# Two of eight channel blocks of a depthwise convolution moved from TensorE to VectorE, in small groups of taps

## The chip, the cores and the metric

The kernel runs on one core of a Trainium2 chip. The metric is the device time of one execution in microseconds (us); the median of three runs of the kernel before is 2086.12 us (2085.93 to 2087.42). TensorE (PE in the profile, PEld for its weight loads) multiplies matrices, VectorE (DVE) and ScalarE (ACT) work element by element, SyncE (SP) issues the DMA transfers.

## The reference

One inference step of a small decoder: a prompt of 512 positions and 8 sample sequences of 8 positions each, 1024 channels, all in float32. The change concerns the convolution module, the first layer:

```python
def conv_module(x, prev, norm_g, w_in, b_in, w_dw, b_dw, ln_g, ln_b, w_out, b_out):
    u = rms_norm(x, norm_g)
    a = u @ w_in + b_in
    glu = a[..., :D_MODEL] * jax.nn.sigmoid(a[..., D_MODEL:])
    ext = jnp.concatenate([prev.astype(glu.dtype), glu], axis=1)
    c = lax.conv_general_dilated(ext, w_dw[:, None, :].astype(ext.dtype), window_strides=(1,),
                                 padding='VALID', dimension_numbers=('NWC', 'WIO', 'NWC'),
                                 feature_group_count=D_MODEL) + b_dw
    h = jax.nn.silu(layer_norm(c, ln_g, ln_b))
    return h @ w_out + b_out, ext[:, -(CONV_WIDTH - 1):]
```

A depthwise convolution of 31 taps: every output channel is a sum of 31 shifted copies of its own input channel, each times a weight of the channel, plus a bias. A layer norm over the channels follows. After this layer come a feed-forward part, an attention layer over three dilated windows and a second feed-forward part; the change leaves them as they are.

## The kernel before

Channels lie on partitions: 8 blocks c = 0 to 7 of 128 channels. The positions, 512 of the prompt and 64 of the samples, N = 576, lie along the free dimension. They are projected in two halves of 288 (`HN`).

The work around the change is one loop, `for c in range(1, KT + 1)` at L628, which overlaps block c's projection with block c-1's convolution. The order of the instructions on each engine is the order in which the code emits them; nothing reorders them later. An iteration emits:

- `diagonals(c)` (L546, VectorE): the 31 taps of block c as diagonal matrices of 32x32, for TensorE.
- `in_proj(c, 0)` (L511): the first half of the projection. It begins with `w_next` (L161), which has SyncE load a later weight (`w_load`, L122 and L125, 1 MB), issues one or two copies of cache data from DRAM to DRAM behind it (`bg_copy`, L184, 1 MB each), and splits the weight that has arrived into a high part on ScalarE (`whi`, L140, four instructions) and a low part on VectorE (`wlo`, L141, four). A weight load waits on SyncE's queue until the split before has released the buffer, and the copies behind it wait too. Then TensorE multiplies 2 x 24 times, first the gate, then the value, each into a bank of its own of accumulator memory (`inp`, two banks). ScalarE takes the sigmoid of the gate (`sg`, L529), VectorE adds the bias and multiplies (`ext`, L536). The sigmoid frees the gate's bank, `ext` the value's; the next half needs both.
- `samples(c - 1, 0, 16)` (L578): the convolution of the 64 sample positions. ScalarE writes 31 products (`prod`, L586 and L588), 16 here and 15 after the convolution; VectorE sums them when the last is there (L590).
- `conv(c - 1)` (L551): the prompt's convolution on TensorE, 124 matmuls of 32x32 by 32x512 in four row groups, each two instructions in the trace. Its four banks (`acc`) are copied to SBUF by ScalarE and VectorE (`ev`, L561 and L563).
- In iteration 3, `pilot()` (L592): the mean over the channels of blocks 0 and 1, a first estimate of the layer norm's mean. It is subtracted from every block ahead of the sums. Then the squares of these blocks on ScalarE (`square`, L604).
- From iteration 4 on, `sums` (L608): TensorE adds up an earlier block and its squares, for the layer norm.
- `in_proj(c, 1)`: the second half; its `ext` completes the input of `conv(c)`.
- `reduced(c - 1)` (L565): TensorE adds up the four row groups of the convolution, VectorE adds the bias and subtracts the pilot mean into `cT` (L571, L573, L574).

After the loop the layer norm is completed from the sums (L657 on), and the output projection follows.

Of the kernel before, what the change touches and what calls it, by code (L numbers as in the profile page):

```python
# [30 lines left out]
ALU = mybir.AluOpType  # L31
# [3 lines left out]
KT = 8  # L35
S = 512
NB = 8
T = 8
NS = NB * T
# [8 lines left out]
TAPS = 31  # L48
# [42 lines left out]
def trunk(ctx: ExitStack, tc: tile.TileContext, I, O, dbg=None):  # L91
    nc = tc.nc
# [64 lines left out]
    def w_work(n=100):  # L157
        for _ in range(min(n, len(parts))):
            parts.pop(0)()

    def w_next(lazy=False):  # L161
        w_work()
        while not wstate["ready"]:
            if not wstate["raw"]:
                w_load()
            w_split()
            w_work()
        r = wstate["ready"].pop(0)
        if not lazy:
            w_load()  # L170
        bg_copy()
        w_split()
        if not lazy:
            w_work()
        return r
# [41 lines left out]
    ones = const.tile([128, 128], F32, name="ones")  # L217
# [127 lines left out]
    def conv_layer():  # L345
        with ExitStack() as cx:
            big = cx.enter_context(tc.tile_pool(name="a_big", bufs=1))
            wk = cx.enter_context(tc.tile_pool(name="a_wk", bufs=2))
            def row(tag, name):
                return wk.tile([128, N], F32, tag=tag, name=name)  # L350
# [4 lines left out]
            wdT = big.tile([128, KT, TAPS], F32, name="wdT")  # L355
# [7 lines left out]
            with tc.tile_pool(name="a_ps0", bufs=1, space=PSUM, reuse_waits="tile") as ps:  # L363
# [11 lines left out]
                o = 0  # L375
# [19 lines left out]
                def xtile():  # L395
                    return ps.tile([128, 512], F32, tag="xp", name="xp", bufs=3)
# [4 lines left out]
                for r in range(5):  # L401
                    n = 128 if r < 4 else NS
# [25 lines left out]
                for r in range(5):  # L428
                    n = 128 if r < 4 else NS
                    dg = wk.tile([128, 128], F32, name="dg", bufs=4)  # L430
                    nc.vector.tensor_scalar(dg[:n], ident[:n], rn[:n, r:r + 1], None, op0=ALU.mult)
                    o = pr[:, 0, r * 128:(r + 1) * 128] if r < 4 else pr[:, 1, :NS]
                    nc.tensor.matmul(o, ones[:n], dg[:n, :n], start=r in (0, 4), stop=r in (3, 4))
                pt = xtile()
# [16 lines left out]
                for k in range(KT):  # L451
# [9 lines left out]
                    for i, pt in ((1, pg), (0, pa)):  # L461
                        for h in range(2):
                            c = slice(h * HN, (h + 1) * HN)
# [6 lines left out]
                pt = xtile()  # L470
# [4 lines left out]
                for k in range(0, KT, 2):  # L475
                    pt = xtile()
# [12 lines left out]
            def bank(tag, n):  # L489
                return ps.tile([128, 512], F32, tag=tag, name=tag, bufs=n)  # L490

            cv = cvx.enter_context(tc.tile_pool(name="a_cv", bufs=1))
            cT = cv.tile([128, KT, N], F32, name="cT")
            tails = cv.tile([128, KT, 96], F32, name="tails")
            pil = cv.tile([128, N], F32, name="pil")
            exf = [cv.tile([128, 30 + S], F32, name=f"ext{i}") for i in range(KT)]
# [3 lines left out]
            bdw = V["a_b_dw"]  # L500
# [5 lines left out]
            hs = [slice(h * HN, (h + 1) * HN) for h in range(2)]  # L506
            grp = [slice(32 * r, 32 * r + 32) for r in range(4)]
            SP = S - HN
            W, SG = {}, {}

            def in_proj(c, h):  # L511

                if h == 0:
                    SG[c] = row("a", "sg")
                if c:
                    if h == 0:
                        W[c] = w_next(lazy=c == KT - 1)
                    wh, wl = W[c]
                    pts = []
                    for i in (1, 0):  # L520
                        pt = bank("inp", 2)[:, :HN]
                        for k in range(KT):
                            mm3(pt, wh[:, k, i], wl[:, k, i], uh[:, k, hs[h]], ul[:, k, hs[h]], k == 0, k == KT - 1)
                        pts.append(pt)
                    pg, pa = pts
                else:
                    pg, pa = pg0[:, h], pa0[:, h]
                sg = SG[c][:, hs[h]]
                nc.scalar.activation(sg, pg, AF.Sigmoid, bias=V["a_b_in"][:, 8 + c:9 + c])  # L529
                e, b = exf[c], V["a_b_in"][:, c:c + 1]  # L530
                jobs = [(e[:, 30:30 + HN], pa, sg)] if h == 0 else [
                    (e[:, 30 + HN:], pa[:, :SP], sg[:, :SP]),
                    (exts[:, c, :, 30:], pa[:, SP:].rearrange("p (b t) -> p b t", b=NB),
                     sg[:, SP:].rearrange("p (b t) -> p b t", b=NB))]
                for o, x, g in jobs:
                    nc.vector.scalar_tensor_tensor(o, x, b, g, op0=ALU.add, op1=ALU.mult)  # L536
                if h:
                    nc.scalar.activation(tails[:, c, 0:30], e[:, S:], AF.Copy)
                    nc.scalar.activation(tails[:, c, 32:].rearrange("p (b t) -> p b t", b=NB), exts[:, c, :, 30:], AF.Copy)
# [6 lines left out]
            def diagonals(c):  # L546
                d = DG[c] = cv.tile([128, TAPS, 32], F32, name="dgs", bufs=2)
                nc.vector.tensor_mul(d, id32[:, None, :].to_broadcast([128, TAPS, 32]),
                                     wdT[:, c, :, None].to_broadcast([128, TAPS, 32]))

            def conv(c):  # L551
                acc = [bank("acc", 4) for _ in range(4)]
                for m in range(0, TAPS, 4):
                    for j in range(m, min(m + 4, TAPS)):
                        for r, g in enumerate(grp):
                            nc.tensor.matmul(acc[r][32 * (j - m):32 * (j - m) + 32], DG[c][g, j], exf[c][g, j:S + j],  # L556
                                             start=m == 0, stop=j + 4 >= TAPS)
                ev = EV[c] = cv.tile([128, 4, S], F32, name="ev")
                for r in range(4):
                    if r % 2:  # L560
                        nc.vector.tensor_copy(ev[:, r], acc[r])  # L561
                    else:
                        nc.scalar.activation(ev[:, r], acc[r], AF.Copy)  # L563

            def reduced(c):  # L565
                pt, ev = bank("red", 1), EV.pop(c)
                for r, g in enumerate(grp):
                    nc.tensor.matmul(pt[g], id32, ev[:, r], start=True, stop=True)
                o, b = cT[:, c, :S], bdw[:, c:c + 1]
                if c < 2:  # L570
                    nc.vector.tensor_scalar(o, pt, b, None, op0=ALU.add)  # L571
                else:
                    nc.vector.scalar_tensor_tensor(o, pt, b, pil[:, :S], op0=ALU.add, op1=ALU.subtract)  # L573
                    nc.vector.tensor_sub(cT[:, c, S:], cT[:, c, S:], pil[:, S:])  # L574
# [17 lines left out]
            def pilot():  # L592

                for h in range(2):
                    pt = bank("inp", 2)[:, :HN]
                    for k in range(2):
                        nc.tensor.matmul(pt, ones, cT[:, k, hs[h]], start=k == 0, stop=k == 1)
                    nc.scalar.activation(pil[:, hs[h]], pt, AF.Copy, scale=1.0 / 256)
                for k in range(2):
                    nc.vector.tensor_sub(cT[:, k], cT[:, k], pil)  # L600

            SQ, STB = {}, []

            def square(c):  # L604
                SQ[c] = wk.tile([128, N], F32, tag="sq3", name="sq", bufs=3)
                nc.scalar.activation(SQ[c], cT[:, c], AF.Square)

            def sums(c):  # L608

                if not STB:  # L610
                    STB.append(bank("stat", 1))
                sq = SQ.pop(c)
                for q, x in enumerate((cT[:, c, :S], sq[:, :S], cT[:, c, S:], sq[:, S:])):
                    nc.tensor.matmul(STB[0][grp[q], :S if q < 2 else NS], ones[:, :32], x, start=c == 0, stop=c == KT - 1)

            def state_rows(hf):
                pt = bank("inp", 2)
# [4 lines left out]
                for a, n, d in ((0, 30, O["conv_state_prompt"][0, 0]), (32, 64, O["conv_state_sample"][0, :, 22:30])):  # L622
                    nc.sync.dma_start(d[..., hf * 512:(hf + 1) * 512], st[a:a + n])

            diagonals(0)
            for h in range(2):
                in_proj(0, h)
            for c in range(1, KT + 1):  # L628
                diagonals(c) if c < KT else None
                if c < KT:  # L630
                    in_proj(c, 0)
                else:
                    w_load()
                    w_work()
                    state_rows(0)
                samples(c - 1, 0, 16)
                conv(c - 1)
                samples(c - 1, 16, TAPS)
                if c == 3:
                    pilot()  # L640
                    square(0)
                    square(1)
                for k in (0, 1, 2) if c == 4 else (c - 2,) if c > 4 else ():
                    sums(k)
                if c < KT:
                    in_proj(c, 1)
                else:
                    nc.scalar.preload_act_table_set("natural_log_exp_and_others")
                    nc.sync.dma_start(O["conv_state_sample"][0, :, :22, :], I["cache_conv"][0, :, 8:, :])
                    state_rows(1)  # L650
                reduced(c - 1)
                if c >= 3:
                    square(c - 1)
            sums(KT - 1)


            mu, q, v, y = pil, row("a", "q"), row("b", "v"), row("a", "y")  # L657
# [49 lines left out]
            for m0 in range(0, KT, 2):  # L707
# [4 lines left out]
                for i in range(2):  # L712
                    m, pt = m0 + i, pts[i]
# [838 lines left out]
```

## Time and profile before

| what | value |
|---|---|
| median of three runs | 2086.12 us |
| the profiled execution, its own time | 2083.47 us |
| its span in the profile | 2081.5 us |
| convolution loop, iterations 1 to 7 | 44.3 to 232.6 us of the span |
| granted TensorE clock, mean over the span | 0.981 |

The profile shows one execution. A row of a group of instructions gives line, engine, operation and tiles (written from read), the number, the busy time in us and the mean duration in ns, and then the idle time of the engine ahead of them with what ended it. A row of the chain of waits gives start and length in us and what the end of the kernel depended on at that time; "issue" is time in which the engine waited for nothing that the profile shows. A timeline row gives start, length, engine, line and operation; consecutive instructions of one kind are merged with their count, and a bracket holds the idle time ahead. The row of a stretch gives start and end, length, the busy time of PE, PEld, DVE, ACT and POOL with their numbers of instructions, the granted TensorE clock (1 is full speed), the DMA engines' share and GB/s.

### The profile page before, as it was taken

Reading aid. Unit: us, or ns where it says so; the run is one execution under the profiler, and the core shown is the slowest. Engines: PE = TensorE matmul, PEld = TensorE weight load, DVE = VectorE, ACT = ScalarE, POOL = GpSimd, SP = SyncE. Lnnn points to the kernel's source line nnn. Section 1 sums busy time; section 2 is a strip of 40 time slices with the busy share of each in tenths; the row PEclk is TensorE's granted clock in tenths of the full one; section 3 lists DMA queues with packets and bytes.
Section 4 is the critical chain, followed back from the end, with each engine's and each line's share of the span. In section 5 each row is a group of like instructions: output and inputs, shape, how many; then the busy total and the mean of one; then the engine's idle time right before and its main releaser. Section 6 shows DMA issues by size and latency. Waiting matters only on the chain.

```text
span 2081.5 us, 41730 instructions
## 1 busy us (share of the span) xinstructions
PE 1972.3 (95%) x17621; PEld 1808.7 (87%) x17621; DVE 974.0 (47%) x1868; ACT 813.0 (39%) x1840; POOL 159.8 (8%) x292
## 2 busy tenths in 40 slices
PE   6989799999999999999999999989797999999999
PEld 6657499999999999998889889866565999999998
DVE  5333485432443478465356356325354554324432
ACT  6434554221222344344344344347563332212222
POOL 1000000000000024032022012000012000000000
PEclk9999999999999999999999999989988999999999
DMA  7322066657655855768778877889978665543222
GB/s 209 110 94 102 23 225 226 206 212 277 202 202 183 302 187 161 236 178 237 226 218 223 253 212 212 259 185 227 211 174 209 225 221 195 203 128 82 75 71 74
DMA packets 368877, 387.88 MB, mean 186 GB/s; under 512 B 17983, under 2 KB 357975, under 8 KB 367010
## 3 DMA queue, kind: packets, MB, share of 16 engines
q1 hardware_dynamic: 368130, 384.06, 61.5%
q8 instruction: 139, 2.28, 0.5%
q0 software_dynamic: 560, 1.14, 0.2%
q14 instruction: 48, 0.39, 0.1%
HBM read 348.07 MB, written 146.86 MB: 238 GB/s over the span
## 4 chain that ended last, share of the span: by engine, by line
PE 86%; DMA 6%; ACT 3%; DVE 2%; SPq 2%; issue 1%; another core or an unknown queue 0%; ACTq 0%; DVEq 0%
PE pmm L230 13%; PE pmm L229 13%; PE pmm L228 13%; PE pj L228 7%; PE pj L229 6%; PE pj L230 6%; PE acc L556 3%; PE pj L1147 3%; PE tp L920 3%; PE pmp L229 2%; PE pmp L230 2%; PE pmp L228 2%; PE inp L228 2%; PE tp L945 2%; PE pv L1018 1%; PE inp L229 1%
## 5 line engine op out<-in xcount | busy, mean ns | idle before, releaser
L230 PE MATMUL pmm<-uh,wlo 128*128 128x288 f32 x1344 | 396.2, 295 | 0.0
L228 PE MATMUL pmm<-uh,whi 128*128 128x288 f32 x1344 | 395.9, 295 | 0.0
L229 PE MATMUL pmm<-ul,whi 128*128 128x288 f32 x1344 | 395.7, 294 | 0.0
L228 PE MATMUL pj<-whi,xh 128*128 128x256 f32 x1152 | 331.5, 288 | 0.9 <-DVE xT L766 0.9
L229 PE MATMUL pj<-wlo,xh 128*128 128x256 f32 x1152 | 322.0, 279 | 0.0
L230 PE MATMUL pj<-whi,xl 128*128 128x256 f32 x1152 | 321.7, 279 | 0.0
L229 PEld LDWEIGHTS pmm<-ul,whi 128*128 128x128 f32 x1344 | 252.1, 188 | 0.1
L228 PEld LDWEIGHTS pmm<-uh,whi 128*128 128x128 f32 x1344 | 252.1, 188 | 0.1
L230 PEld LDWEIGHTS pmm<-uh,wlo 128*128 128x128 f32 x1344 | 252.1, 188 | 0.0
L228 PEld LDWEIGHTS pj<-whi,xh 128*128 128x128 f32 x1152 | 216.4, 188 | 10.3 <-issue 9.5
L140 ACT ACTIVATE whi<-wraw 128x1024 fp32r<-128x1024 f32 (+3 forms) x206 | 169.2, 871 | 123.8 <-PE pmm L229 100.6
L229 PEld LDWEIGHTS pj<-wlo,xh 128*128 128x128 f32 x1152 | 216.4, 188 | 0.0
L230 PEld LDWEIGHTS pj<-whi,xl 128*128 128x128 f32 x1152 | 215.9, 187 | 0.0
L141 DVE TENSOR_TENSOR wlo<-wraw,whi 128x1024 fp32r<-128x1024 f32 (+3 forms) x206 | 197.8, 1003 | 24.3 <-ACT whi L140 24.1
L228 PE MATMUL pmm<-hh,whi 128*128 128x288 f32 x704 | 207.6, 295 | 0.0
L230 PE MATMUL pmm<-hh,wlo 128*128 128x288 f32 x704 | 207.5, 295 | 0.0
L229 PE MATMUL pmm<-hl,whi 128*128 128x288 f32 x704 | 207.2, 294 | 0.0
L755 DVE TENSOR_TENSOR gt<-pmm,rs 128x576 f32<-128x576 f32 x42 | 31.8, 758 | 224.5 <-PE pmm L230 224.5
L271 ACT ACTIVATE hh<-gt 128x576 fp32r<-128x576 f32 x44 | 30.2, 687 | 263.3 <-DVE gt L756 263.3
L229 PEld LDWEIGHTS pmm<-hl,whi 128*128 128x128 f32 x704 | 132.1, 188 | 0.0
L228 PEld LDWEIGHTS pmm<-hh,whi 128*128 128x128 f32 x704 | 132.1, 188 | 0.0
L230 PEld LDWEIGHTS pmm<-hh,wlo 128*128 128x128 f32 x704 | 132.0, 188 | 0.0
(292 smaller groups left out, 3510.0 us busy)
## 6 DMA issues: line engine op xcount, KB each, us to landing
out_dram<-in_cache_kv_w_dram SPq DMA_DIRECT2D x64, 1016.0 KB
wraw<-in_w_gate_up_dram SPq DMA_DIRECT2D x88, 512.0 KB
out_dram<-in_cache_kv_w_dram SPq DMA_DIRECT2D x32, 1008.0 KB
wraw<-in_w_kv_dram SPq DMA_DIRECT2D x24, 1024.0 KB
wraw<-in_w_down_dram SPq DMA_DIRECT2D x32, 704.0 KB
kk<-in_cache_kv_w_dram SPq DMA_DIRECT2D x40, 512.0 KB
vv<-in_cache_kv_w_dram SPq DMA_DIRECT2D x40, 512.0 KB
scr<-r SPq DMA_DIRECT2D x36, 512.0 KB
```

The lines of the kernel that those rows point to most:

```text
L140: nc.scalar.activation(hi[:, c], raw[:, c], AF.Copy)
L141: wstate["lo"].tensor_sub(lo[:, c], raw[:, c], hi[:, c].bitcast(F32))
L228: nc.tensor.matmul(out, wh, xh, start=start, stop=False)
L229: nc.tensor.matmul(out, wh, xl, start=False, stop=False)
L230: nc.tensor.matmul(out, wl, xh, start=False, stop=stop)
L271: nc.scalar.activation(hi, x, AF.Copy)
L556: nc.tensor.matmul(acc[r][32 * (j - m):32 * (j - m) + 32], DG[c][g, j], exf[c][g, j:S + j], start=m == 0, stop=j + 4 >= TAPS)
L755: nc.vector.tensor_mul(halves(t2), pu, halves(rs))
L920: nc.tensor.transpose(pt[:, j * 128:(j + 1) * 128], Z["k", n][:, j, i * 128:(i + 1) * 128], ident)
L945: nc.tensor.matmul(pt[32 * bi:32 * bi + 32, a:a + n], q[:, x, i, b], kn[:, x, i, T * b:T * b + T] if k is None else k[:, i, bi], start=i = ...
L1018: nc.tensor.matmul(pvt[r], ph[:n, ti, r], v[:n, bi], start=ti == 0, stop=ti == 9)
L1147: nc.tensor.matmul(pt[:, :CW], xs[:, k], x[:, k], start=k == 0 and x is wh, stop=k == KT - 1 and x is wl)
```

## The change

Blocks 0 and 3 (`DVB`) are convolved on VectorE: one instruction multiplies the input by the first tap and adds the bias, and 30 more each add one shifted input times its tap to the result. `diagonals`, `conv` and `reduced` are not emitted for these blocks. The 31 instructions come from a generator (`taps`). `run(4)`, `run(3)` and `run(4)` emit eleven of them per iteration at three places: after `in_proj(c, 0)` and the first sample products, after the rest of the sample products and their sum, and after `in_proj(c, 1)`. Block 0's taps are emitted in iterations 1 to 3 (11, 11, 9), block 3's in 4 to 6 (11, 11, 9). The pilot mean is that of blocks 1 and 2 (`PILOT`), and it is formed in iteration 4 in place of 3. The pilot is subtracted from a VectorE block as soon as its taps are done and the pilot exists (`block`): from block 0 at the end of iteration 4, from block 3 at the end of iteration 6. The sums of a block are emitted in the iteration after its squares: of 1, 2 and 0 in iteration 5, of 4 in 6, of 5 and 3 in 7. The samples' part of the convolution stays as it was for all blocks.

```diff
+            DVB, PILOT = (0, 3), (1, 2)
...
-                if c < 2:
+                if c in PILOT:
                     nc.vector.tensor_scalar(o, pt, b, None, op0=ALU.add)
...
+            def taps(c):
+
+                o = cT[:, c, :S]
+                nc.vector.tensor_scalar(o, exf[c][:, :S], wdT[:, c, 0:1], bdw[:, c:c + 1], op0=ALU.mult, op1=ALU.add)
+                for j in range(1, TAPS):
+                    yield
+                    nc.vector.scalar_tensor_tensor(o, exf[c][:, j:j + S], wdT[:, c, j:j + 1], o,
+                                                   op0=ALU.mult, op1=ALU.add)
+                done.append(c)
...
+            def run(n):
+                while n > 0 and work:
+                    if next(work[0], 0) == 0:
+                        work.pop(0)
+                    n -= 1
+
+            def block(c):
+
+                nc.vector.tensor_sub(cT[:, c], cT[:, c], pil)
+                square(c)
...
             for c in range(1, KT + 1):
-                diagonals(c) if c < KT else None
+                if c - 1 in DVB:
+                    work.append(taps(c - 1))
+                if c < KT and c not in DVB:
+                    diagonals(c)
...
                 samples(c - 1, 0, 16)
-                conv(c - 1)
+                run(4)
+                if c - 1 not in DVB:
+                    conv(c - 1)
                 samples(c - 1, 16, TAPS)
-                if c == 3:
+                run(3)
+                if c - 1 == PILOT[1] + 1:
                     pilot()
-                    square(0)
-                    square(1)
-                for k in (0, 1, 2) if c == 4 else (c - 2,) if c > 4 else ():
-                    sums(k)
+                    for k in PILOT:
+                        square(k)
+                    ready.extend(PILOT)
+                elif c - 1 > PILOT[1] + 1:
+                    while ready:
+                        sums(ready.pop(0))
...
-                reduced(c - 1)
-                if c >= 3:
-                    square(c - 1)
-            sums(KT - 1)
+                run(4)
+                if c - 1 not in DVB:
+                    reduced(c - 1)
+                    if c - 1 not in PILOT:
+                        square(c - 1)
+                        ready.append(c - 1)
+                if c == KT:
+                    run(1000)
+                if c - 1 > PILOT[1]:
+                    while done:
+                        block(done[0])
+                        ready.append(done.pop(0))
+            ready.sort(key=lambda k: k == KT - 1)
+            for k in ready:
+                sums(k)
```

More of the change, by code (lines that the diff above doesn't have):

```diff
@@ L595, in pilot @@
                     pt = bank("inp", 2)[:, :HN]
-                    for k in range(2):
-                        nc.tensor.matmul(pt, ones, cT[:, k, hs[h]], start=k == 0, stop=k == 1)
+                    for i, k in enumerate(PILOT):
+                        nc.tensor.matmul(pt, ones, cT[:, k, hs[h]], start=i == 0, stop=i == 1)
                     nc.scalar.activation(pil[:, hs[h]], pt, AF.Copy, scale=1.0 / 256)
-                for k in range(2):
+                for k in PILOT:
                     nc.vector.tensor_sub(cT[:, k], cT[:, k], pil)
@@ L613, in sums @@
                 for q, x in enumerate((cT[:, c, :S], sq[:, :S], cT[:, c, S:], sq[:, S:])):
-                    nc.tensor.matmul(STB[0][grp[q], :S if q < 2 else NS], ones[:, :32], x, start=c == 0, stop=c == KT - 1)
+                    nc.tensor.matmul(STB[0][grp[q], :S if q < 2 else NS], ones[:, :32], x, start=c == PILOT[0], stop=c == KT - 1)
             def state_rows(hf):
@@ L623, in state_rows @@
                     nc.sync.dma_start(d[..., hf * 512:(hf + 1) * 512], st[a:a + n])
-            diagonals(0)
             for h in range(2):
                 in_proj(0, h)
+            def taps(c):
[6 more added lines that the diff above has]
+                done.append(c)
+            work, done = [], []
+            def run(n):
[6 more added lines that the diff above has]
+                square(c)
+            ready = []
             for c in range(1, KT + 1):
-                diagonals(c) if c < KT else None
+                if c - 1 in DVB:
+                    work.append(taps(c - 1))
+                if c < KT and c not in DVB:
+                    diagonals(c)
                 if c < KT:
@@ L636, in conv_layer @@
                 samples(c - 1, 0, 16)
-                conv(c - 1)
+                run(4)
+                if c - 1 not in DVB:
+                    conv(c - 1)
                 samples(c - 1, 16, TAPS)
-                if c == 3:
+                run(3)
+                if c - 1 == PILOT[1] + 1:
                     pilot()
-                    square(0)
-                    square(1)
-                for k in (0, 1, 2) if c == 4 else (c - 2,) if c > 4 else ():
-                    sums(k)
+                    for k in PILOT:
+                        square(k)
[3 more added lines that the diff above has]
+                        sums(ready.pop(0))
                 if c < KT:
```

## The prediction, before the result was known

> **What bounds the kernel now.** I read the engine totals first, then the stage that the diff touches, cut at the starts of its iterations, then the chain of waits inside it.
>
> ```profile
> span 2081.5 us, 41730 instructions
> PE 1972.3 (95%) x17621; PEld 1808.7 (87%) x17621; DVE 974.0 (47%) x1868; ACT 813.0 (39%) x1840; POOL 159.8 (8%) x292
> ```
>
> TensorE is busy for 95% of the span, VectorE for 47%. Work that leaves TensorE counts if the same iteration doesn't find another end. The busy times by stretch, one row for each of the iterations c=1 to 7 of the convolution loop:
>
> ```profile
> 44.33:68.10 23.77, 23.01 (x353) 18.26 (x353) 11.29 (x14) 14.13 (x44) 0.00 (x0) 1.00 0.64 211
> 68.10:95.73 27.63, 24.49 (x353) 17.63 (x353) 9.18 (x12) 12.13 (x41) 0.00 (x0) 0.94 0.34 115
> 95.73:126.28 30.55, 25.11 (x361) 18.70 (x361) 13.14 (x17) 14.34 (x47) 0.00 (x0) 1.00 0.22 70
> 126.28:157.00 30.72, 27.82 (x378) 18.79 (x377) 10.74 (x13) 12.80 (x43) 0.00 (x0) 0.94 0.30 103
> 157.00:185.33 28.33, 25.32 (x361) 18.55 (x361) 10.65 (x13) 12.80 (x43) 0.00 (x0) 0.94 0.41 148
> 185.33:208.98 23.65, 23.65 (x362) 18.07 (x361) 10.06 (x12) 12.29 (x41) 0.00 (x0) 1.00 0.14 47
> 208.98:232.63 23.65, 23.65 (x361) 18.08 (x362) 8.02 (x10) 10.72 (x38) 0.00 (x0) 1.00 0.01 2
> ```
>
> The columns are the length, then the busy time of PE, PEld, DVE and ACT. The last two iterations are TensorE alone, 23.65 us; VectorE is busy 8 to 13 us in each. The iterations c=2 to 5 are 4 to 7 us longer. The chain of waits says why:
>
> ```profile
> 44.33 0.40 PE inp L228
> 50.92 8.56 PE acc L556 x232
> ...
> 67.10 1.00 PE red L568 x8
> ...
> 74.61 5.44 PE acc L556 x148
> 80.05 3.14 issue
> ...
> 113.57 1.08 ACT ev L563 x2
> 114.66 3.62 ACT prod L586 x15
> 118.27 0.30 ACT pil L598
> ```
>
> Half a projection is 50.9 - 44.3 = 6.5 us, a convolution 8.6, a reduction 1.0; what is left of 23.65 is 0.95 for the sums. In c=2 the convolution stops for 3.14 us at "issue", that is, for nothing the profile shows. In c=3 TensorE also waits 5 us, from 113.6 to 118.6, until ScalarE has copied two accumulators, multiplied 15 sample products and written the pilot mean.
>
> The stops are the second quantity. The same happens in c=3, 4 and 5 (TensorE's timeline, then one stretch after a stop):
>
> ```profile
> 61.37 0.40 PE L229 MATMUL inp<-ul,whi 128*128 128x288 f32 x1 [0.76 <-issue]
> ...
> 111.22 2.30 PE L556 MATMUL acc<-ext,dgs 32*32 32x512 f32 x58 [2.48 <-issue]
> ...
> 174.07 1.14 PE L556 MATMUL acc<-ext,dgs 32*32 32x512 f32 x27 [3.01 <-issue]
> ```
> ```profile
> 83.19:88.14 4.95, 4.95 (x91) 1.95 (x90) 0.00 (x0) 0.00 (x0) 0.00 (x0) 0.66 0.01 3
> ```
>
> After the stop the granted clock is 0.66: 91 matmuls take 4.95 us instead of 91 x 8.6/248 = 3.15. A stop so costs about 3 + 1.8 us, which is the excess of c=2 over 23.65 - 0.95. An iteration is 352 matmuls with as many weight loads, 704 instructions. A convolution has 248 of the matmuls (352 less 96 and 8). The stops lie 158 (5.45 us at 29 a us), 248 - 58 = 190 and 248 - 27 = 221 into it in c=2, 3 and 5: 704 + 2 x 32 = 768 instructions from the first to the second. The small gap in c=1 lies some 510 before the first. Both are multiples of about 256, so I take the stops for late arrival of a block of 256 instructions. Each stop comes some microseconds after SyncE has issued a weight load with cache copies behind it:
>
> ```profile
> 50.73 1.00 SPq L125 DMA_DIRECT2D wraw<-in_a_w_in_dram  x2
> ...
> 72.71 0.99 SPq L125 DMA_DIRECT2D wraw<-in_a_w_in_dram  x2
> ...
> 101.41 1.00 SPq L125 DMA_DIRECT2D wraw<-in_a_w_in_dram  x2
> ...
> 161.89 0.37 SPq L122 DMA_DIRECT2D wraw<-in_a_w_out_dram  x1
> 162.30 1.86 SPq L184 DMA_DIRECT2D out_dram<-in_cache_kv_w_dram  x3
> ```
>
> If a block is asked for when its predecessor is entered, 128 matmuls earlier, the requests fell at 75.7, 104.4 and 166.8 (the convolutions start 6.5 us into the iteration): 3.0, 3.0 and 4.9 us after the weight load was issued, and all came late, 9.8 to 12.2 us after that issue. In c=1 it fell about when the load was issued (50.8 against 50.73), and came in time. [...]
>
> **The change, part by part.** *Removed:* for blocks 0 and 3 a convolution and a reduction each, 2 x (8.6 + 1.0) = 19.2 us of TensorE, and their copies, diagonals and evictions. That is 2 x 512 instructions, two whole blocks each, so the later places of the stops move only with the pilot and the sums. *Added:* on VectorE 62 taps and two subtractions of 0.75 us. *Moved:* the pilot from c=3 to c=4, where no convolution stands before it; nothing is moved on SyncE's queue, but each weight load, and the copies behind it, still waits there for VectorE's last wlo of the iteration before.
>
> A tap is a scalar_tensor_tensor over 128x512, both inputs in SBUF, scalar from a column, reading what the tap before wrote. Nearest rows, by shape and by time:
>
> ```profile
> L268 DVE SCALAR_TENSOR_TENSOR ul<-xk,cols,uh 128x512 fp32r<-128x512 f32 x8 | 5.9, 743 | 0.0
> ...
> L672 DVE TENSOR_SCALAR v<-v 128x512 f32<-128x512 f32 x1 | 0.4, 426 | 0.0
> ```
> ```profile
> 337.70 0.76 DVE L246 TENSOR_TENSOR na<-na,nv 128x576 f32<-128x576 f32 x1
> 338.49 0.76 DVE L247 SCALAR_TENSOR_TENSOR rs<-na,ny 128x576 f32<-128x576 f32 x1
> ```
>
> L268 has the form but not the dependence: 0.743. In the dependent pair the second starts 0.79 after the first, 0.03 over its duration. So 0.78 a tap, 24 us a block; bounds are 0.43 (L672, one input) and 1.18 (L548 below, 992 elements). Eleven taps an iteration are 8.6 us, beside 8 to 13 us busy in 23 or more: VectorE has the time. What counts is its order. The quiet iteration c=6, VectorE then ScalarE:
>
> ```profile
> 186.28 1.18 DVE L548 TENSOR_TENSOR dgs<-id,wdT 128x992 f32<-128x992 f32 x1
> 187.64 2.50 DVE L141 TENSOR_TENSOR wlo<-wraw,whi 128x512 fp32r<-128x512 f32 x4 [0.17 <-ACT whi L140]
> 191.97 0.52 DVE L536 SCALAR_TENSOR_TENSOR ext<-inp,cols,sg 128x288 f32<-128x288 f32 x1 [1.83 <-PE inp L230]
> 200.45 1.29 DVE L561 COPY ev<-acc 128x512 f32<-128x512 f32 x2 [7.96 <-PE acc L556]
> 205.21 3.77 DVE L590 TENSOR_REDUCE cT<-prod 128x64 f32<-128x1984 f32 x1 [3.48 <-ACT prod L586]
> ```
> ```profile
> 186.99 2.18 ACT L140 ACTIVATE whi<-wraw 128x512 fp32r<-128x512 f32 x4
> 189.07 0.48 ACT L529 ACTIVATE sg<-inp,cols 128x288 f32<-128x288 f32 x1
> ...
> 189.78 3.75 ACT L586 ACTIVATE prod<-exts,wdT 128x64 f32<-128x64 f32 x15
> ```
>
> Four taps now stand after the first ext, covered by the convolution; three between the reduction over taps (L590) and the second ext, with no cover; four after it. The second ext frees a projection bank and completes the convolution's input. Where there is no convolution, the 31 sample products (31 x 0.245 = 7.6 us on ScalarE), which it covered, come due as well. I follow the queues by these durations, from 44.3:
>
> - c=1: products 49.9 to 57.6, L590 to 61.3, three taps to 63.6, second ext to 64.2. TensorE ends its halves at 57.4, starts the next gate half when ScalarE's sigmoid has freed the bank, at 58.1, and its value half at 64.2.
> - c=2: conv(1) 67.5 to 76.1, the next half to 82.6, the reduction to 83.6. Weight load issued at 70.9, the request at matmul 30, 68.5: in time.
> - c=3: second ext of c=2 at 87.4, conv(2) 90.65 to 99.25, end 106.8. Load issued at 93.6, request at 92.8: in time, narrowly. The pilot's 5 us are gone from here.
> - c=4: no convolution; first ext at 116.9, products to 121.5, pilot copies to 122.2, so TensorE is idle some 4 us; L590, three taps and the two subtractions to 128.9, then squares, and the second sigmoid at 130.
> - c=5: starts 130.1; conv(4) 136.6 to 145.2. The weight load, with three copies behind it, is issued at 138.4, when the four taps, block 0's subtraction and square, and whi and wlo are done. The sums of c=4 come later now, so a boundary stands at matmul 221 + 24 = 245; the request at 117 falls at 140.65, 2.25 us after the issue. I take it as late, as the one at 3.0 was. Bounds of its cost: 0 and 7.5 us (arrival 12.2 after the issue, 150.6, against 145.1, and 2 for the clock). I take 6, as the last copy may still be behind it.
> - c=6 and 7: TensorE bound, c=7 with one more set of sums.
>
> | c | before | after |
> |---|---|---|
> | 1 | 23.8 | 13.8 |
> | 2 | 27.6 | 25.5 |
> | 3 | 30.6 | 23.2 |
> | 4 | 30.7 | 23.3 |
> | 5 | 28.3 | 25.5 + 6 |
> | 6 | 23.7 | 23.5 |
> | 7 | 23.7 | 24.6 |
>
> The sum is 188.4 against 165.4, a gain of 23 us. The last block and all behind it keep their order and cost, so the gain stays. The profiled execution took 2083.47 (span 2081.5), which gives 2060.5; the median of the runs, 2086.12, is 2.65 above it, so I forecast 2063.
>
> **Rivals.**
> - *No stop in c=5.* If the fetch still gets in 2.25 us after the issue, the 6 us are gained too: 2057. For it: the request lies between one that was in time (0.1) and one that was late (3.0). [...]
> - *A stop in c=3 as well.* Its margin is 0.8 us by my count. It costs 5 to 8 us: 2070.
> - *A dearer tap.* 18 taps (three in each of six iterations) stand uncovered, so each 0.1 us costs 1.8 us. At 1.18, 7 us: 2070. [...]
> - *Slower: VectorE becomes the bound.* Its own work in an iteration is about 10.7 us (c=4) plus 11 taps; over 23 us it sets the pace, from 1.1 us a tap on. Up to there 6 us are lost by the 18 uncovered taps, and each further 0.1 us costs 1.1 us in each of five iterations. The gain of 23 is used up near 1.45 us a tap; at 1.6 the time is 2063 + 6 + 26 = 2095. That is twice L268 and above the upper bound, so it takes a contention that no row shows.
> - *Nothing gained.* TensorE waits in c=1 and c=4 for as long as the convolutions took, if ScalarE's products run late behind other waits: 2086. The busy times of ACT, 12 to 14 us an iteration, speak against it.
>
> **How the numbers follow.** Forecast (one stop, in c=5) 0.44, none 0.27, a stop in c=3 also 0.14, dearer tap 0.08, nothing gained 0.04, slower 0.03. The range from no stop with 3 us to spare (2054) to both stops with a dearer tap (2074) leaves less than 2 in 10 out. A measurement here tells about 0.2%, 4.2 us, from no change: faster 0.93, within 0.04, slower 0.03.
>
> **What would show it.** Right: the second projection half of c=2 starts near 76 and the start that was at 232.6 near 210; taps 0.78 apart; no "issue" stop in the convolutions of c=2 and 3, one near the end of that of c=5; TensorE idle some 4 us before the pilot's bank comes free in c=4. Wrong: taps over 1 us apart, TensorE waiting for ext in every iteration, or stops in c=2 and 3 as before. A start of the last block near 204 would say that the stop in c=5 didn't come.

## The result and the profile after

The changed kernel takes 2063.26 us (median of four runs, 2061.0 to 2065.79) against 2086.02 of the kernel before on the same chip; the ratio is 0.9892, 95% interval 0.9872 to 0.9913. In a second comparison the same two gave 2067.25 and 2084.93, ratio 0.9923 (0.9899 to 0.9947). So the change saves some 16 to 23 us, and the 23 that were forecast lie at the upper end.

The engine totals of the profiled execution after, which took 2061.0 us:

```profile
span 2059.1 us, 40751 instructions
...
PE 1950.8 (95%) x17109; PEld 1801.3 (87%) x17109; DVE 1013.1 (49%) x1922; ACT 810.7 (39%) x1836; POOL 159.9 (8%) x292
```

TensorE has lost 512 matmuls and as many loads, and 21.5 us of busy time; VectorE has gained 39 us. The busy times by iteration, columns as before:

```profile
43.87:57.56 13.69, 12.98 (x97) 12.75 (x97) 8.21 (x14) 13.07 (x42) 0.00 (x0) 1.00 1.08 366
57.56:84.85 27.29, 24.51 (x353) 19.55 (x353) 19.89 (x23) 12.01 (x41) 0.00 (x0) 0.94 0.34 116
84.85:108.20 23.35, 22.87 (x353) 17.92 (x353) 17.00 (x23) 12.00 (x41) 0.00 (x0) 1.00 0.28 91
108.20:130.70 22.50, 17.01 (x105) 15.68 (x105) 19.50 (x25) 12.86 (x43) 0.00 (x0) 0.85 0.40 140
130.70:159.41 28.71, 26.45 (x380) 18.88 (x378) 18.93 (x26) 13.02 (x43) 0.00 (x0) 1.00 0.39 147
159.41:183.06 23.65, 23.65 (x361) 18.08 (x361) 15.77 (x21) 12.58 (x42) 0.00 (x0) 1.00 0.15 47
183.06:207.56 24.50, 24.50 (x370) 18.42 (x370) 12.84 (x17) 11.80 (x41) 0.00 (x0) 1.00 0.01 2
```

The seven iterations take 163.7 us, where 165.4 were forecast and 188.3 were measured before. Each is within 1.8 us of its forecast except c=5 (28.7, not 31.5). TensorE's three longest waits in these iterations, in the view of who waited for whom:

```profile
PE inp L228 <- DVE exts L538: 3.8, 3, 2.8
PE inp L228 <- ACT pil L600: 3.4, 1, 3.4
PE acc L558 <- issue: 2.3, 1, 2.3
```

Total us, times, and the longest. Of the four stops in convolutions one is left, 2.3 us long.

One execution can mislead here, so variants are compared below by a second measure as well: the *loop*, from the first projection matmul of the loop to the first matmul of the output projection (`pmp`). It is 217.4 us before and 192.7 after in these two profiles, and 212.1 and 196.8 in a second pair (e5 and e12), so one kernel's loop varies by 4 to 5 us. What lies behind it took 1820 to 1832 us in the profiles of before, of the change and of its variants, without an edit there (only e1 and e2 issue their copies there); this is the noise that the loop is free of.

### The profile page after: what moved, and what is told of

The parts are those of the page before. It is cut to its first block, busy times and chain, and to the rows that moved or that the text cites. A ratio compares the mean times of both kernels' runs of the same rounds, so it can differ in the third digit from the quotient of the medians.

```text
span 2059.1 us, 40751 instructions
## 1 busy us (share of the span) xinstructions
PE 1950.8 (95%) x17109; PEld 1801.3 (87%) x17109; DVE 1013.1 (49%) x1922; ACT 810.7 (39%) x1836; POOL 159.9 (8%) x292
## 4 chain that ended last, share of the span: by engine, by line
PE 84%; DMA 6%; ACT 5%; DVE 3%; SPq 1%; issue 1%; another core or an unknown queue 0%; ACTq 0%; DVEq 0%
PE pmm L230 13%; PE pmm L229 13%; PE pmm L228 13%; PE pj L228 7%; PE pj L229 7%; PE pj L230 7%; PE pj L1191 3%; PE tp L964 3%; PE acc L558 3%; PE pmp L229 2%; PE pmp L230 2%; PE pmp L228 2%; DMA nat<-scr 2%; PE pv L1062 2%; PE tp L989 2%; DMA vv<-in_cache_kv_w_dram 1%
## 5 line engine op out<-in xcount | busy, mean ns | idle before, releaser
L228 PE MATMUL pmm<-uh,whi 128*128 128x288 f32 x1344 | 395.9, 295 | 0.0
L228 PE MATMUL pj<-whi,xh 128*128 128x256 f32 x1152 | 332.0, 288 | 0.9 <-DVE xT L810 0.9
L228 PEld LDWEIGHTS pmm<-uh,whi 128*128 128x128 f32 x1344 | 252.1, 188 | 0.1
L228 PEld LDWEIGHTS pj<-whi,xh 128*128 128x128 f32 x1152 | 217.2, 189 | 10.3 <-issue 9.5
L141 DVE TENSOR_TENSOR wlo<-wraw,whi 128x1024 fp32r<-128x1024 f32 (+3 forms) x206 | 197.7, 1003 | 23.3 <-ACT whi L140 23.0
L228 PE MATMUL pmm<-hh,whi 128*128 128x288 f32 x704 | 207.6, 295 | 0.0
L228 PEld LDWEIGHTS pmm<-hh,whi 128*128 128x128 f32 x704 | 132.1, 188 | 0.0
```

The source lines that it names most:

```text
L141: wstate["lo"].tensor_sub(lo[:, c], raw[:, c], hi[:, c].bitcast(F32))
L228: nc.tensor.matmul(out, wh, xh, start=start, stop=False)
```

## The experiments

**e1 and e2: no cache copies in the loop.** Both kernels without the copies of the loop. The copies go on behind the loop, so all later ones come later, up to the second feed-forward part.

```diff
                 w_load()
                 bg_copy()
                 w_split()
                 w_work()
+                wstate["rate"] = 0
...
-            wstate["lo"], wstate["cut"] = nc.vector, 2
+            wstate["lo"], wstate["cut"], wstate["rate"] = nc.vector, 2, 1.5
```

> The kernel before, with the cache copies of the convolution loop left for later (their rate is 0 in the loop; the second feed-forward part issues them). Theory: the stops of 2.5 to 3.1 us in c=2 to 5 come from blocks of instructions queued behind weight loads with copies, so they go, and their slow clock with them: about 0.8 + 4.9 + 2.5 + 5.1 + 4.7 = 18 us less, near 2068. The wait for the pilot in c=3 (5 us) stays. Rival, the stops lie in the instruction stream itself or in the weight loads: they stay, 2086.

> The changed kernel with the same edit. Theory: only the stop in c=5 goes (2.27 us and the slow clock behind it), so about 4 us less, near 2059, and without copies the change is worth some 9 us in place of 23: the rest of its gain was the stops. Rival, the gain is that of the removed matmuls alone and the stops were unimportant: the difference between e1 and e2 stays near 23 us.

e1 took 2071.32 us (before: 2083.77), ratio 0.994 (0.9921 to 0.9959); e2 2064.74, ratio 0.9905 (0.9878 to 0.9932). All of TensorE's waits in iterations 1 to 7 of e1:

```profile
PE inp L228 <- ACT pil L599: 3.0, 1, 3.0
PE inp L228 <- ACT exts L483: 1.0, 1, 1.0
```

No "issue" stop is left, while the weight loads still run. That the stops come with the copies is shown. The gain is 12 us, not 18: the loop is 16.7 us shorter than in the first profile of before and 11.5 shorter than in the second (e5), whose stops are smaller. e2 missed its 2059: its loop is 2.5 to 6.6 us shorter than that of the change, but its median lies between the two of the change. Between e1 and e2 the change is worth 6.6 us by the medians and 10.5 by the loops (200.7 and 190.2), where 9 was expected and the rival asked for 23. The two intervals overlap slightly, so the medians alone barely show this gain; that it is below 23 they do show. By the loops, the change is worth 24.7 and 15.3 us with the copies and 10.5 without; between a third and somewhat over a half of its gain, then, is that stops go.

**e3: the instruction stream of before moved by 64.**

```diff
+            pad = bank("red", 1)
+            for i in range(16):
+                nc.tensor.matmul(pad[:32, :32], id32, id32, start=True, stop=True)
             diagonals(0)
```

> The kernel before with 16 small matmuls ahead of the loop that nothing reads, 64 instructions with their weight loads. Theory of blocks of 256 instructions: every block boundary comes 32 matmuls earlier, so the stops stand near matmul 126, 158, 181 and 189 of the convolutions of c=2 to 5, and as they still end when the transfers do, each is about 1 us longer: 2086 + 4 + 1 to 2. Rival, the transfers stop TensorE at a time of their own: the stops stay near 158, 190, 213 and 221, time 2087.

Its one run took 2080.54 us. TensorE's timeline at the stops:

```profile
88.87 0.29 PE L228 MATMUL inp<-uh,whi 128*128 128x288 f32 x1 [2.31 <-issue]
...
109.88 3.36 PE L556 MATMUL acc<-ext,dgs 32*32 32x512 f32 x90 [2.30 <-issue]
...
142.03 2.76 PE L556 MATMUL acc<-ext,dgs 32*32 32x512 f32 x67 [1.59 <-issue]
...
169.03 2.30 PE L556 MATMUL acc<-ext,dgs 32*32 32x512 f32 x59 [0.96 <-issue]
```

The count is what is left of 248 behind the stop: the stops stand at 158, 181 and 189, as expected to the matmul. The stop expected at 126 in c=2 didn't come. By the count of matmuls its request fell 0.7 us after the weight load was issued (76.22); the trace has the block's transfer at 74.5, ahead of the load (how this is read follows under e5). The next boundary, 128 matmuls on, stopped TensorE in the following projection half, behind its sixth matmul (254 - 248 = 6). The blocks of 256 instructions are shown. The lengths, however, went down from the first profile, not up; e5 shows that they vary as much in one kernel, so they don't tell whether a stop ends with the transfers. The rows under e12 do.

**e5: before again.**

> The kernel before, unchanged, for a second profile. Theory: a stop is as long as a block's way takes beyond the 4.4 us in which a convolution uses up the block before; that way took 6.8 to 7.5 us in the first profile and 5.4 to 6.8 in e3, so places stay (158, 190, 213, 221) and lengths vary by 1 to 2 us, and one may be missing. Rival, the stops are the same in every execution, 2.5 to 3.1 us.

```profile
79.18 3.34 PE L556 MATMUL acc<-ext,dgs 32*32 32x512 f32 x90 [0.74 <-issue]
...
103.28 2.30 PE L556 MATMUL acc<-ext,dgs 32*32 32x512 f32 x58 [0.15 <-issue]
...
136.52 3.62 PE L556 MATMUL acc<-ext,dgs 32*32 32x512 f32 x35 [2.69 <-issue]
...
168.40 1.14 PE L556 MATMUL acc<-ext,dgs 32*32 32x512 f32 x27 [2.56 <-issue]
```

The places are the same to the matmul; the lengths are 0.15 to 2.69 us. Counted from where TensorE enters the block before, a stop is what a block's way takes beyond the 4.4 us in which a convolution runs 128 matmuls. By that the way was 6.9 to 7.5 us in the first profile, 4.6 to 7.1 here, 5.4 to 6.7 in e3. The kernel before so has a variable cost of its own, and the profile from which the forecast started is the dearer of the two.

The traces hold these blocks themselves. The page of a profile has a DMA queue of the kind "instruction"; its rows before and after the change give packets, MB and share of time:

```profile
q8 instruction: 139, 2.28, 0.5%
```
```profile
q8 instruction: 135, 2.21, 0.5%
```

A packet is 16.4 KB. TensorE's 2 x 17621 instructions are 138 blocks of 256, and the 1024 that the change removes are the four packets that are gone. Narrow windows of the DMA view place each packet in time. In the first profile of before, the packets of the four late blocks start at 80.9, 108.9, 140.7 and 171.6, which is 4.6 to 5.3 us after TensorE entered the block before. They take 0.92 to 1.15 us each, and TensorE goes on 1.2 to 1.5 us after their end. The packet that follows each of these stops, with no copies in flight, starts 1.1 us after TensorE goes on. So a stop is shown to be the wait for a block whose transfer starts late. That a packet can start before TensorE's own entry, as in e3 (74.5 against 76.9), says that requests run ahead of the matmuls executed; by how much isn't shown.

**e4: the pilot alone.** `DVB = ()`, with block 0 treated as a block without pilot, and its subtraction and square at the end of iteration 5.

> All eight blocks on TensorE; only the pilot mean is from blocks 1 and 2 and formed in iteration 4, block 0's subtraction at the end of iteration 5. Theory: the wait of 5 us before the pilot moves from c=3 to c=4 and nothing is gained, within 3 us of 2086. Rival, moving the pilot is what frees iteration 3: 2081.

2082.20 us, ratio 0.9996 (0.9976 to 1.0016). The stop of c=5 stood at 248 - 3 = 245, as worked out for the later sums. The pilot's move gains nothing by itself.

**e8: block 3 alone.**

```diff
-            DVB, PILOT = (0, 3), (1, 2)
+            DVB, PILOT = (3,), (0, 1)
...
+            diagonals(0)
             for h in range(2):
                 in_proj(0, h)
```

> Only block 3 on VectorE; pilot from blocks 0 and 1 in iteration 3, as before. Theory: c=4 loses its convolution, its reduction and its stop (9.6 and 4.9 us) and gains some 2 us of waits for ScalarE and VectorE: 10 to 13 us less, 2072. Rival, by removed matmuls alone half of the whole gain, which is 11.5: the time can't tell these apart, the iteration can (c=4 from 30.7 to about 18).

2067.11 us, ratio 0.9916 (0.9895 to 0.9938), 17.5 us less. From conv(2) to conv(4) it is 47.8 us, 61.7 in e5: 13.9 less in the place that was meant, somewhat more than expected (c=4 takes 15.7 us, where about 18 was). The loop is 196.2 us against 192.7 and 196.8 with both blocks. Block 0, as the change does it, so adds no more than the loops vary by: its convolution is replaced by waits, which the next experiment takes away.

**e6 and e11: three taps later.** The taps that stand ahead of the second `ext` go behind it.

```diff
                 samples(c - 1, 16, TAPS)
-                run(3)
...
-                run(4)
+                run(7)
                 if c - 1 not in DVB:
                     reduced(c - 1)
```

> The changed kernel with the three taps between the sum over taps and the second ext moved behind that ext (4, 0 and 7 in place of 4, 3 and 4). Theory: TensorE's waits for ext (2.8 us in c=1, about 0.5 in c=2 and 3) go, and with the first the slow clock of the half behind it (1.6): about 5 us less, 2058. Rival, the taps' order doesn't matter as VectorE has time anyway: 2063.

> e6 unchanged, on the same chip as e9 and e10, and a second profile of it. Theory: 2054.5 within 3 us and again no stop in the convolutions of c=2, 3 and 5, as the weight loads are issued behind the requests for the next block. Rival, e6's profile was a lucky one: a stop of 2 us or more in one of them.

2054.53 us, ratio 0.9848 (0.9812 to 0.9885), and again 2054.80, ratio 0.9848 (0.9822 to 0.9873). The loop is 182.6 and 182.7 us, 10 and 14 less than in the two profiles of the change. TensorE's waits in iterations 1 to 7 of e6:

```profile
PE inp L599 <- DVE ext L538: 2.5, 1, 2.5
PE inp L228 <- ACT pil L600: 1.0, 1, 1.0
PE inp L228 <- ACT exts L482: 1.0, 1, 1.0
PE inp L228 <- ACT sg L531: 0.7, 1, 0.7
PE inp L228 <- DVE exts L538: 0.5, 1, 0.5
```

The wait for `exts` fell from 3.8 to 0.5 us, that for the pilot from 3.4 to 1.0, while that for the second `ext` rose from 1.6 to 2.5. No stop is left, in either profile, which is more than expected. In c=5 seven taps, where four stood, are now between that `ext` and VectorE's wlo, and delay with it the weight load. It is issued at 135.41 where conv(4) starts at 131.06, and its copies from 135.83 on: the request at matmul 117 falls at 135.1, ahead of them. The trace has the block's packet at 135.3. In e9, e10 and e11, which keep this order, no stop comes either. This version beats both kernels.

**e7: the second half ahead of the last samples.** From the changed kernel; in the last iteration the order stays.

```diff
-                samples(c - 1, 16, TAPS)
-                run(3)
+                if c == KT:
+                    samples(c - 1, 16, TAPS)
...
                     in_proj(c, 1)
+                    samples(c - 1, 16, TAPS)
...
-                run(4)
+                run(7)
```

> The changed kernel with the second projection half (and in iteration 4 the pilot) emitted ahead of the last 15 sample products and their sum, the three taps behind them. Theory: in c=1 and c=4 TensorE waits for ScalarE's 31 products and VectorE's sum; with the sigmoid and ext ahead of them c=1 takes 13 us in place of 14, conv(1) starts 5 us earlier, the pilot waits for 16 products only and c=4 takes 16 to 18 us in place of 23: 10 to 15 us less, 2048 to 2053. Rival, VectorE is then late everywhere: the gain is under 4 us.

2066.20 us, ratio 0.99 (0.9865 to 0.9934): no gain over the change. Two of TensorE's waits in its loop, which the change doesn't have:

```profile
PE red L570 <- ACT ev L565: 5.3, 1, 5.3
PE inp L599 <- DVE cT L573: 5.0, 1, 5.0
```

Half of the theory held: conv(1) starts 19.2 us after the loop's first matmul, against 24.8 and 23.2 in the two profiles of the change. But the sum over taps and the taps behind it now lie late in VectorE's queue, and what TensorE needs stands behind them: in c=4 the pilot waits 5.0 us for block 2's last step, and in the last iteration a reduction waits 5.3 us for an eviction behind late sample products. What c=1 gained in this way was lost again in these waits.

**e9 and e10, both from e6.** e9 puts the squares of blocks 1 and 2 behind the second half of iteration 4. e10 moves a third block:

```diff
-            DVB, PILOT = (0, 3), (1, 2)
+            DVB, PILOT = (0, 3, 6), (1, 2)
...
-                run(4)
+                run(9 if c == KT - 1 else 4)
                 if c - 1 not in DVB:
                     conv(c - 1)
+                if c == KT:
+                    run(4)
...
-                run(7)
+                run(9 if c == KT - 1 else 7 if c < KT else 0)
```

> e6 with the squares of blocks 1 and 2 behind the second projection half of iteration 4 instead of ahead of it. Theory: the sigmoid of that half, which frees the gate's bank for c=5, no longer waits for the sum over taps and two subtractions on VectorE; c=5 starts some 2 us earlier: 2052 where e6 had 2054.5, at the edge of what a measurement tells. Rival, the bank isn't what c=4 waits for: no change against e6.

> e6 with block 6 on VectorE too: its taps in iterations 7 (9 and 9) and 8 (4, 4 and the last 5 behind the last reduction). Theory: 9.6 us of TensorE go from c=7, but c=7 then waits 1 to 2 us for the products and the sum, and 5 taps, a subtraction, a square and a set of sums (3.9 + 0.75 + 0.7 + 0.95 us) come after the last convolution, with no cover: 1 to 3 us less than e6. Rival, each block moved is worth what the first two were, 9 to 10 us: 2045.

e9: 2056.73 us, ratio 0.9859 (0.9834 to 0.9884), no difference from e11: the 2 us expected didn't come. e10: 2052.06 us, ratio 0.9837 (0.9809 to 0.9865), against e11's 0.9848 on the same chip. The medians are 2.7 us apart, inside both intervals, and e10's loop is 1.5 us longer, not shorter (184.2): a gain isn't shown. The stretch of its last iterations, columns as above:

```profile
165.00:218.00 53.00, 36.39 (x441) 26.40 (x437) 47.53 (x59) 30.00 (x99) 0.00 (x0) 0.93 0.07 22
```

VectorE is busy 47.5 of 53 us, TensorE 36.4. VectorE is nearly the bound here, as in the rival of that name, but by more taps and not by dearer ones.

**e12: the change again.**

> The changed kernel once more, for a second profile. Theory: the stop of c=5 stands at matmul 245 of 248 again and lasts 1 to 3 us, as the block's way is 5.4 to 7.5 us after a request at 117 and 4.4 of them are covered; the first pmp matmul comes 190 to 194 us after the first matmul of the loop. Rival, the first profile caught a short one, and 6 us as predicted is the rule.

The chain of waits of the first profile after, then TensorE's timeline in e12:

```profile
145.81 2.27 issue
148.08 1.04 PE acc L558 x3
```
```profile
150.11 1.91 PE L558 MATMUL acc<-ext,dgs 32*32 32x512 f32 x3 [2.62 <-issue]
```

The stop stands at 245 in both and lasts 2.27 and 2.62 us. From conv(4) to conv(5) it is 28.6 and 32.2 us, 25.4 in e6 without a stop: with what follows it the stop costs 3.3 and 6.8 us. The loop, 196.8 us, missed its expected 190 to 194. Most of the difference is the clock. The stretches behind the stop, of the first profile after and of e12, have a granted clock (third column from the end) of 1.00 and of 0.50:

```profile
148.10:152.00 3.90, 3.90 (x29) 1.14 (x29) 0.69 (x1) 3.30 (x13) 0.00 (x0) 1.00 0.71 271
```
```profile
150.10:154.00 3.90, 3.89 (x21) 0.97 (x22) 0.69 (x1) 2.85 (x11) 0.00 (x0) 0.50 0.74 271
```

The last column is GB/s: in both the transfers still run at 271 GB/s after the block has come. That a stop ends with the transfers, as e3's expectation had it, is wrong.

## Why the prediction was right

- *What bounds the loop* was right: e1 shows the stops to come with the copies, e3 and the fetched packets the blocks of 256 instructions. One reading was off without harm to the sum: of the 5 us in c=3 in which TensorE was said to wait for ScalarE, it was idle for 3.0 (L228, `pil`); the pilot's own matmuls fill the rest (TensorE is busy 2.09 of the 5.03 us from 113.57). They left c=3 together.
- *The taps* were right. VectorE's timeline in c=1 after the change shows three taps in 2.33 us from the first start to the last end: 0.79 from start to start and 0.75 for the last. Other rows of that size are close: L141, a plain TENSOR_TENSOR, takes 0.68 (mean of 25), and L268 needed 0.743.

```profile
51.57 2.33 DVE L635 SCALAR_TENSOR_TENSOR cT<-ext,wdT,cT 128x512 f32<-128x512 f32 x3
57.15 3.68 DVE L592 TENSOR_REDUCE cT<-prod 128x64 f32<-128x1984 f32 x1 [3.26 <-ACT prod L588]
60.75 2.31 DVE L635 SCALAR_TENSOR_TENSOR cT<-ext,wdT,cT 128x512 f32<-128x512 f32 x3
62.98 0.45 DVE L538 SCALAR_TENSOR_TENSOR ext<-inp,cols,sg 128x224 f32<-128x224 f32 x1
```

- *The order* was right: the same rows show products to 57.1, the sum over taps, three taps without cover and then `ext` at 63.0, where 63.6 was forecast from a start 0.5 later. c=4 has its 3.4 us of TensorE waiting for the pilot copies (4 forecast).
- *A term was missing:* the slow clock after waits that aren't stops. TensorE waited 2.78 us for `exts` in c=1 and 3.4 for the pilot in c=4, and the stretches behind these waits ran slow:

```profile
63.76:68.63 4.87, 4.87 (x24) 4.71 (x24) 4.76 (x7) 4.87 (x16) 0.00 (x0) 0.65 0.00 0
122.70:126.50 3.80, 3.80 (x16) 3.80 (x17) 3.80 (x2) 0.21 (x1) 0.00 (x0) 0.52 0.80 343
```

  24 matmuls took 4.87 us where 3.25 was counted; after the pilot the clock is 0.52. The first is most of the 1.8 us by which c=2 came out longer. In this profile the clock is 0.50 from 64.93 to 68.34 and from 119.54 to 126.37: the first stretch begins 1.2 us after its wait, the second 0.25 us into it. In e12 the same wait of 2.78 us in c=1 was followed by 24 matmuls in 3.32 us, and the convolution behind them took 8.6: no slow clock. After the stops of 2.27 and 2.62 us in c=5, too, the clock stayed at 1.00 once and fell to 0.50 once. What decides between the two isn't shown.
- *The stop in c=5* came at matmul 245 and in no other convolution, as forecast. That a block is asked for when TensorE enters the block before was an estimate from the places of the stops, and no run shows it: the packet starts 4.6 to 5.3 us after that entry at the four stops before, 4.3 in c=5 after the change (145.69), and 2.4 ahead of it in e3. The length of the stop was taken too long. The upper bound had the block arrive 12.2 us after the issue, and the 6 us stay near it. The block came 148.08 - 139.21 = 8.9 us after, with transfers in flight. What runs through the profiles is the way, stop plus 4.4 us: 6.7 and 7.0 here, 4.6 to 7.5 elsewhere. That the 6 us lie between the 3.3 and 6.8 measured is partly luck: in e12 the slow clock made up for the shorter stop. The last block started at 207.6, between the 210 of the forecast and the 204 that stood for no stop.
- *The gain of 23 us* was right by size within what two measurements say, 22.8 and 17.7 us. It was counted against a profile of before with four long stops; against the loop of e5 the same count gives some 18. In the sum of the iterations two misses cancel in part: c=2 came out 1.8 us longer than forecast and c=5 2.8 shorter. So close a match is partly luck.
- *The rivals:* no stop in c=5 is what e6 reached by another order. A stop in c=3, a dearer tap, slower and nothing gained didn't come; VectorE came near to being the bound with a third block (e10).

## What to carry to other kernels

When work goes to an idle engine, its busy share says that it fits; its place in that engine's queue says what it costs. Put it behind whatever frees a bank or feeds the busy engine, not ahead: the same 62 taps gave 8.7 us more by the first measurement of the change, and 12.7 by the second, when three of each eleven moved behind `ext`; a part of this is the stop in c=5, which went with it. And a dense stretch of short matmuls needs its instructions in time: a stop at "issue", at a fixed count of instructions, while bulk copies run, was gone where the next block's transfer started ahead of the copies (e6: 135.3 against 135.83; e9 to e11, with the same order, had no stop either).

## What was not expected of the hardware

At the stops of the convolutions, a block of 256 instructions took 4.6 to 7.5 us from TensorE's entry into the block before it, with cache copies in flight, against 4.4 us of cover. Without the copies no stop was left in the kernel before (e1), and one of 0.18 us after the change (e2). Behind the stop of 2.62 us in e12 the granted clock was 0.50 over 3.9 us and 0.66 over the next 4.0, and with both the stretch from conv(4) to conv(5) took 32.2 us, against 25.4 in e6 without a stop. Behind the wait of 2.78 us in c=1 after the change it was 0.65 over 4.87 us. Behind the same wait in e12 24 matmuls took 3.32 us, at full speed, and behind the stop of 2.27 us after the change the clock was 1.00 over 3.9 us. What makes the difference isn't shown.
